# Two engines without work wait for the last load instead of ending at once, in a ReLU-and-row-sum kernel

## The chip, the cores and the metric

The kernel runs on one core of a Trainium2 chip. The metric is the device time of one execution in microseconds; lower is better. Every execution also has a span: the time from the first to the last instruction of the kernel in its profile. The device time was 1.3 to 1.7 us longer than the span in the kernels that nothing held up at their end, and this case is about what lies in that difference. All executions quoted here were at a granted clock of 1.0.

## The reference

```python
def setup_inputs():
    batch, seq, dim = 32, 512, 1024
    return {"x": np.random.randn(batch, seq, dim).astype(np.float32)}

def reference(x):
    relu_x = np.maximum(x, 0)
    return np.sum(relu_x, axis=-1).astype(np.float32)
```

The input is 32 x 512 x 1024 x 4 bytes = 67.1 MB, the output 64 KB. Every input byte is read once.

## The kernel before

SyncE issues all loads and stores. ScalarE and VectorE do the arithmetic. TensorE and GpSimd get no work, apart from four small constant fills on GpSimd and the barrier at the start, both of which the framework adds. Seven loads of 8.39 MB go through three buffers; the rest is loaded in shrinking pieces, so that little is left to compute when the last piece lands.

```python
    n_in = NBIG + len(TAIL) + 2
    s_in = [nc.alloc_semaphore(f"s_in{i}") for i in range(n_in)]   # one for each load
    # ... the other semaphores ...
    for c in range(NBIG + 1):
        if c >= NB:
            sp.wait_ge(s_dve, 3 * (c - NB + 1))        # buffer free again
        if c < NBIG:
            g, j = CHUNKS[c]
            sp.dma_start(out=buf[:, c % NB, :, :], in_=xv[g][:, j : j + BIG, :]).then_inc(
                s_in[c], 16
            )
    # ... the shrinking loads; the last one: ...
    sp.dma_start(out=last[:, 0 : LAST[1]], in_=xv[-1][:, BIG - 1, LAST[0] : D]).then_inc(
        s_in[-1], 16
    )
    # ... wait for two flags, then the first store (112 of 128 columns) ...

    # ... ScalarE: relu, VectorE: sum, for six big loads; after that rows are shared out ...
    act.wait_ge(s_in[-2], 16)
    on_act(buf[:, tb, BIG - 1, 0 : LAST[0]], last[:, LAST[1] : LAST[1] + 1]).then_inc(s_tact, 1)
    dve.wait_ge(s_tact, 1)
    dve.wait_ge(s_in[-1], 16)
    on_dve(last[:, :], res[:, J - 1 : J]).then_inc(s_tdve, 1)

    sp.wait_ge(s_tdve, 1)
    sp.dma_start(out=ov[-1][:, :], in_=res[:, start[-1] : J]).then_inc(s_out, 16)
    sp.wait_ge(s_store, 16 * (len(REGIONS) - 1))
    sp.wait_ge(s_out, 16)
```

Of the kernel before, what the change touches and what calls it, by code (L numbers as in the profile page):

```python
# [2 lines left out]

P = 128
D = 1024
BIG = 16
NTWO = 6
NB = 3
REGIONS = [112, 16]
CHUNKS = [(0, 0), (0, 16), (0, 32), (0, 48), (0, 64), (0, 80), (0, 96)]  # L10
STEPS = [4, 5, 7]
MIXED = [3, 4, 5]
TAIL = [8, 4, 2, 1]
LAST = [512, 512]


def bass_relu_sum_kernel(
    nc: bass.Bass,
    x: bass.AP,
    out: bass.AP,  # L20
):







    fp32 = mybir.dt.float32
    ALU = mybir.AluOpType  # L30
    AF = mybir.ActivationFunctionType
    X = mybir.AxisListType.X

    B, S, _ = x.shape
    J = B * S // P
    NBIG = len(CHUNKS)
    assert BIG * NBIG + sum(TAIL) + 1 == J == sum(REGIONS) and sum(LAST) == D

    xr = x.rearrange("b s d -> (b s) d")
    of = out.rearrange("b s -> (b s)")  # L40
    start = [sum(REGIONS[:i]) for i in range(len(REGIONS))]
    xv = [
        xr[P * s : P * (s + n), :].rearrange("(p j) d -> p j d", p=P)
        for s, n in zip(start, REGIONS)
    ]
    ov = [of[P * s : P * (s + n)].rearrange("(p j) -> p j", p=P) for s, n in zip(start, REGIONS)]

    buf = nc.alloc_sbuf_tensor("buf", [P, NB, BIG, D], fp32)
    last = nc.alloc_sbuf_tensor("last", [P, LAST[1] + 1], fp32)
    res = nc.alloc_sbuf_tensor("res", [P, J], fp32)  # L50

    n_in = NBIG + len(TAIL) + 2
    s_in = [nc.alloc_semaphore(f"s_in{i}") for i in range(n_in)]
    s_act = nc.alloc_semaphore("s_act")
    s_dve = nc.alloc_semaphore("s_dve")
    s_fact = nc.alloc_semaphore("s_fact")
    s_fdve = nc.alloc_semaphore("s_fdve")
    s_tact = nc.alloc_semaphore("s_tact")
    s_tdve = nc.alloc_semaphore("s_tdve")
    s_store = nc.alloc_semaphore("s_store")  # L60
    s_out = nc.alloc_semaphore("s_out")

    sp, act, dve = nc.sync, nc.scalar, nc.vector


    tb = NBIG % NB
    for c in range(NBIG + 1):
        if c >= NB:
            sp.wait_ge(s_dve, 3 * (c - NB + 1))
# [5 lines that stand above are left out]
    r = 0  # L75
    tail = []
    for i, n in enumerate(TAIL):
        sp.dma_start(out=buf[:, tb, r : r + n, :], in_=xv[-1][:, r : r + n, :]).then_inc(  # L78
            s_in[NBIG + i], 16
        )  # L80
        tail.append((r, n, s_in[NBIG + i]))
        r += n
    sp.dma_start(out=buf[:, tb, r, 0 : LAST[0]], in_=xv[-1][:, BIG - 1, 0 : LAST[0]]).then_inc(
        s_in[-2], 16
    )
    sp.dma_start(out=last[:, 0 : LAST[1]], in_=xv[-1][:, BIG - 1, LAST[0] : D]).then_inc(
        s_in[-1], 16
    )
    sp.wait_ge(s_fact, 1)
    sp.wait_ge(s_fdve, 1)  # L90
    for g in range(len(REGIONS) - 1):
        sp.dma_start(
            out=ov[g][:, :], in_=res[:, start[g] : start[g] + REGIONS[g]]
        ).then_inc(s_store, 16)


    def on_act(t, acc):
        return act.activation(t, t, AF.Relu, accum_out=acc)  # L98

    def on_dve(t, acc):  # L100
        return dve.tensor_scalar(  # L101
            out=t, in0=t, scalar1=0.0, scalar2=None, op0=ALU.max, op1=ALU.add, accum_out=acc
        )

    def row(c, i):
        return buf[:, c % NB, i, :], res[:, c * BIG + i : c * BIG + i + 1]

    for c in range(NTWO):
        b, steps = c % NB, STEPS if c < NTWO - 1 else MIXED
        act.wait_ge(s_in[c], 16)  # L110
        if steps is MIXED:
            dve.wait_ge(s_in[c], 16)
            for i in (BIG - 4, BIG - 3):
                on_dve(*row(c, i))
        r = 0
        for i, n in enumerate(steps):
            t = buf[:, b, r : r + n, :]
            act.activation(t, t, AF.Relu).then_inc(s_act, 1)  # L118
            dve.wait_ge(s_act, 3 * c + i + 1)
            dve.tensor_reduce(  # L120
                out=res[:, c * BIG + r : c * BIG + r + n], in_=t, axis=X, op=ALU.add
            ).then_inc(s_dve, 1)
            r += n
        if steps is MIXED:
            for i in (BIG - 2, BIG - 1):
                on_act(*row(c, i))


    j0 = NBIG * BIG
    for c in range(NTWO, NBIG):  # L130
        act.wait_ge(s_in[c], 16)
        dve.wait_ge(s_in[c], 16)
        for i in range(BIG):
            ins = (on_act if i % 2 else on_dve)(*row(c, i))
            if i >= BIG - 2:
                ins.then_inc(s_fact if i % 2 else s_fdve, 1)
    for r, n, s in tail:
        if n > 1:
            act.wait_ge(s, 16)
        dve.wait_ge(s, 16)  # L140
        for i in range(r, r + n):
            f = on_act if (i - r) % 2 else on_dve
            f(buf[:, tb, i, :], res[:, j0 + i : j0 + i + 1])
# [14 lines that stand above are left out]
# [1 line left out]
_INS = ['x']  # L159
_OUTS = [((32, 512), 'float32')]  # L160


# [21 lines left out]
```

## Time and profile before

| | before |
|---|---|
| device time, median of 3 | 162.47 us (162.46 to 162.5) |
| span of the profiled execution | 160.7 us |
| device time of the same execution | 162.37 us |
| DMA queue, share of 16 engines' span | 97.4% |
| VectorE, ScalarE busy | 76%, 63% |

The page of the profile, lines of its parts 1 and 3 (busy time and share of the span; packets, MB, share of the engines):

```profile
span 160.7 us, 145 instructions
...
DVE 122.0 (76%) x56; ACT 101.0 (63%) x55; POOL 0.2 (0%) x4
...
q1 hardware_dynamic: 2160, 67.18, 97.4%
HBM read 67.11 MB, written 0.07 MB: 418 GB/s over the span
```

The queue has work nearly all the time. TensorE does not appear, and GpSimd (POOL) has 0.2 us of work at the start. So the loads bound the kernel. The chain of work that ended last is made of loads for the most part. Some 27% of it is ScalarE and VectorE, since SyncE issues a load only when VectorE has freed its buffer; the loads issued before it keep the queue at work meanwhile. The columns are start, length and what it was:

```profile
by line: DMA buf<-in_x_dram 69.2%; ACT buf L118 17.5%; DVE res L120 9.5%; SPq L78 1.0%; ACT buf L98 0.5%; DVE last L101 0.4%; issue 0.3%; SPq L72 0.2%
...
1.17 40.75 DMA buf<-in_x_dram
...
41.94 14.05 ACT buf L118 x3
...
56.01 7.63 DVE res L120
...
63.66 36.31 DMA buf<-in_x_dram
...
123.55 34.19 DMA buf<-in_x_dram
157.74 0.02 issue
157.76 0.73 ACT buf L98 x2
158.49 0.03 issue
158.53 0.69 DVE last L101 x2
```

The timeline of the last two microseconds (start, length, engine, line, operation) and SyncE's longest wait there:

```profile
157.76 0.63 ACT L98 ACTIVATE buf<-buf 128x512 f32<-128x512 f32 x1 [0.83 <-DMA buf<-in_x_dram]
...
158.53 0.69 DVE L101 TENSOR_SCALAR_CACHE_REDUCE last<-last 128x513 f32<-128x513 f32 x1 [0.21 <-ACT buf L98]
159.14 0.08 DVE L101 DVE_READ_ACCUMULATOR last<-last 128x1 f32 x1
159.25 0.34 SPq L153 DMA_DIRECT2D out_dram<-res  x1
```
```profile
SPq L155 <- DMA out_dram<-res: 1.1, 1, 1.1
```

After the last load there is one short reduction and the last store; SyncE then waits 1.1 us for the store, and the span ends at 160.71.

The profile's views stop there, but the trace's semaphore records go on. A semaphore is a counter that engines and transfers count up and that engines wait on; the records show when each one was counted up or cleared. Semaphore 2 belongs to the system's barrier. These are its counts in the trace of before, after the kernel's start, in us:

```
first barrier, way in:   0.943  158.593  158.631  159.367  160.829
first barrier, way back: 160.873  160.911  160.945  160.994
all semaphores from 7 to 255 cleared, in five groups: 160.954 to 161.720
second barrier:          161.810  161.844  161.883  161.927  161.950  162.049  162.087  162.121  162.168
```

The Trainium skill, page "Runtime: NRT & Kernel Launch", section "The ~15µs preamble/postamble breakdown", describes the barrier ahead of a kernel as a chain through the five engines with about 44 ns for each of 8 hops (a hop is the step from one count to the next), and lists for the end of a kernel a barrier, a reset of the semaphores and another barrier. The trace agrees in form: there are nine counts, which is one for each engine on the way in and one for each of the first four on the way back, and the hops of the way back are 34 to 49 ns. An engine counts only when the engine before it in the chain has counted. ScalarE's last instruction ended at 158.485, VectorE's at 159.222 and SyncE's at 160.712; the counts at 158.593, 159.367 and 160.829 follow these by 0.11 to 0.15 us. The counts at 0.943 and 158.631 are then those of the two engines without work.

### The profile page before, as it was taken

How to read it: one execution, taken by the hardware profiler on the slowest of the kernel's cores; microseconds unless marked ns; L12 is line 12 of the kernel's file. 1: busy time of each engine (PE TensorE's matmuls, PEld its weight loads, DVE VectorE, ACT ScalarE, POOL GpSimd, SP SyncE). 2: the span in 40 equal slices, each digit the busy share in tenths (PEclk: the TensorE clock that was granted, in tenths of full speed). 3: DMA queues.
4: the chain of work that ended last, by engine and by line, in shares of the span. 5: the costliest groups of instructions: out<-in, count | busy, mean ns of one | idle time of the engine just before them, and what ended most of it. 6: DMA issues, size and time to landing. Idle time of an engine off the chain costs nothing.

```text
span 160.7 us, 145 instructions
## 1 busy us (share of the span) xinstructions
DVE 122.0 (76%) x56; ACT 101.0 (63%) x55; POOL 0.2 (0%) x4
## 2 busy tenths in 40 slices
DVE  0000004998969898898969989699899999598995
ACT  3000039991599907997099951999329980496972
POOL 0000000000000000000000000000000000000000
DMA  8969969969969969969969969969969969899993
GB/s 261 522 261 522 522 261 522 522 261 522 522 261 522 522 261 522 522 261 522 522 261 522 522 261 522 522 261 522 522 261 522 506 277 522 367 416 391 418 399 113
DMA packets 2160, 67.18 MB, mean 418 GB/s; under 512 B 496, under 2 KB 496, under 8 KB 880
## 3 DMA queue, kind: packets, MB, share of 16 engines
q1 hardware_dynamic: 2160, 67.18, 97.4%
HBM read 67.11 MB, written 0.07 MB: 418 GB/s over the span
## 4 chain that ended last, share of the span: by engine, by line
DMA 69%; ACT 18%; DVE 10%; SPq 1%; issue 0%
DMA buf<-in_x_dram 69%; ACT buf L118 17%; DVE res L120 9%; SPq L78 1%; ACT buf L98 0%; DVE last L101 0%; SPq L72 0%
## 5 line engine op out<-in xcount | busy, mean ns | idle before, releaser
L120 DVE TENSOR_REDUCE res<-buf 128x4 f32<-128x4096 f32 (+3 forms) x18 | 100.4, 5604 | 34.3 <-ACT buf L118 34.3
L118 ACT ACTIVATE buf<-buf 128x4096 f32<-128x4096 f32 (+3 forms) x18 | 80.8, 4553 | 47.1 <-DMA buf<-in_x_dram 47.1
L98 ACT ACTIVATE buf<-buf 128x1024 f32<-128x1024 f32 (+1 forms) x18 | 18.4, 1021 | 9.7 <-DMA buf<-in_x_dram 9.7
L101 DVE TENSOR_SCALAR_CACHE_REDUCE buf<-buf 128x1024 f32<-128x1024 f32 x18 | 21.0, 1215 | 2.7 <-DMA buf<-in_x_dram 2.5
L98 ACT ACTIVATION_READ_ACCUMULATOR buf<-buf 128x1 f32 x18 | 3.4, 186 | 0.0
L118 ACT ACT_TABLE_LOAD x1 | 1.3, 1283 | 0.7 <-PEq L169 0.7
L101 DVE DVE_READ_ACCUMULATOR buf<-buf 128x1 f32 x18 | 1.5, 83 | 0.0
L101 DVE TENSOR_SCALAR_CACHE_REDUCE last<-last 128x513 f32<-128x513 f32 x1 | 0.7, 690 | 0.2 <-ACT buf L98 0.2
L169 POOL MEMSET const-bfloat16-1.0<- 128x1 bf16 x1 | 0.1, 102 | 0.0
L169 POOL MEMSET const-uint8-127<- 128x1 uint8 x1 | 0.1, 102 | 0.0
L169 POOL MEMSET const-float32-0.0<- 128x1 f32 x1 | 0.1, 99 | 0.2 <-issue 0.2
L169 POOL MEMSET const-float32-1.0<- 128x1 f32 x1 | 0.1, 99 | 0.0
L101 DVE DVE_READ_ACCUMULATOR last<-last 128x1 f32 x1 | 0.1, 83 | 0.0
## 6 DMA issues: line engine op xcount, KB each, us to landing
buf<-in_x_dram SPq DMA_DIRECT2D x1, 4096.0 KB, 26.7
buf<-in_x_dram SPq DMA_DIRECT2D x1, 2048.0 KB, 31.2
buf<-in_x_dram SPq DMA_DIRECT2D x1, 1024.0 KB, 33.2
buf<-in_x_dram SPq DMA_DIRECT2D x1, 512.0 KB, 34.0
buf<-in_x_dram SPq DMA_DIRECT2D x1, 256.0 KB, 34.2
last<-in_x_dram SPq DMA_DIRECT2D x1, 256.0 KB, 34.3
buf<-in_x_dram SPq DMA_DIRECT2D x7, 36.3
out_dram<-res SPq DMA_DIRECT2D x1, 56.0 KB, 10.6
```

Of the source, the lines that this page charges most:

```text
L78: sp.dma_start(out=buf[:, tb, r : r + n, :], in_=xv[-1][:, r : r + n, :]).then_inc(s_in[NBIG + i], 16)
L98: return act.activation(t, t, AF.Relu, accum_out=acc)
L101: return dve.tensor_scalar(out=t, in0=t, scalar1=0.0, scalar2=None, op0=ALU.max, op1=ALU.add, accum_out=acc)
L118: act.activation(t, t, AF.Relu).then_inc(s_act, 1)
L120: dve.tensor_reduce(out=res[:, c * BIG + r : c * BIG + r + n], in_=t, axis=X, op=ALU.add).then_inc(s_dve, 1)
L169: nc = _bacc.Bacc("TRN2", target_bir_lowering=False, num_devices=1)
```

## The change

Its intent: TensorE and GpSimd, which have nothing to do, should not run on to the end of their streams while the loads are on, but wait inside the kernel until the last load has landed.

```diff
@@ after the first store is issued
             out=ov[g][:, :], in_=res[:, start[g] : start[g] + REGIONS[g]]
         ).then_inc(s_store, 16)
 
+    for idle in (nc.tensor, nc.gpsimd):
+        idle.wait_ge(s_in[-1], 16)
```

Nothing else changes. The order of instructions on every engine is the same, and the program has one more instruction on each of the two engines. Line numbers of the changed kernel are shifted by 1 to 4.

## The prediction

> What bounds the kernel. Loads do. The page of the profile gives the one DMA queue 97.4% of the 160.7 us span and 418 GB/s; VectorE is busy 76%, ScalarE 63%. In the trace's semaphore records the 8.39 MB chunks complete 19.35 us apart (22.1, 41.45, 60.8, ... us), which is 433.6 GB/s. The Trainium skill ("DMA: Bandwidth & Descriptors", section "Where 436 GB/s comes from") names 435.2 GB/s as the ceiling of the ports into on-chip memory; the trace agrees. After the last load only a short tail remains (timeline): the last load is complete at 158.41, VectorE's last work runs 158.53 to 159.22, the store is issued at 159.25, complete at 160.67, and SyncE's final wait ends the span at 160.71. The reported time of the profiled run is 162.37 us.
>
> What the change does. It removes nothing and adds one semaphore wait to TensorE and one to GpSimd. The instruction order on VectorE, ScalarE and SyncE and all loads stay as they were. The two engines write no buffer, so no buffer comes free at another time and no transfer moves. A released wait of this kind takes 17 to 51 ns in the trace (start barrier).
>
> What it can touch: only the closing sequence that the system runs after the kernel. The Trainium skill ("Runtime: NRT & Kernel Launch", section "The ~15us preamble/postamble breakdown") lists a barrier over the five engines that passes from engine to engine at about 44 ns a hop, a reset of the semaphores, and another barrier. The trace shows it. The barrier's semaphore is counted up at 0.94 us (one engine that had nothing to do), 158.593 (108 ns after ScalarE's last instruction), 158.631 (the other idle engine, 38 ns later), 159.367 (145 ns after VectorE's last), 160.829 (117 ns after SyncE's last), then back in hops of 34 to 49 ns until 160.994; semaphores are cleared from 160.95 to 161.72, and the second barrier runs from 161.81 to 162.17.
>
> On the critical path? With the change the two idle engines are released at 158.41, when the last load's semaphore reaches 16, plus about 30 ns (VectorE's own wait on that semaphore ended at 158.435), and reach the barrier some 0.15 us later, an estimate from the 108 to 145 ns seen above: about 158.55 to 158.60. ScalarE gets there at 158.593, so the first three steps move by 0 to 0.1 us. VectorE arrives only at 159.367 and SyncE at 160.829, so there are about 0.7 and 2.2 us of slack. Nothing of it reaches the end. Waiting at one semaphore instead of at the barrier's frees no resource that the kernel uses.
>
> Predicted time: 162.45 us, range 162.15 to 162.8; the rest is scatter between runs (before: 0.04 us) and chips, and possibly a tenth of a microsecond if the closing sequence starts differently. Faster by over 2%: 1%; within 2%: 98%; slower by over 2%: 1%.
>
> What would show it right or wrong. Span 160.6 to 160.8 us, chunk spacing 19.35 us, the tail's 158.41 to 160.71 unchanged within 0.1 us, two new waits ending near 158.45 on TensorE and GpSimd; the barrier's first count moves from 0.94 to about 158.6, its fifth stays about 0.12 us after SyncE's last wait, and reported time less span stays about 1.7 us.
>
> What would make it wrong: [...] the engine that clears its semaphores last (161.43 to 161.72) starts sooner or later because it waited elsewhere; or engines that end at once disturb the loads in a way that this trace doesn't show, which the chunk spacing near the ceiling speaks against.

## The result, and the profile after

| | before | after |
|---|---|---|
| device time, median of 6 | 162.47 us (162.19 to 162.53) | 162.21 us (161.94 to 162.4) |
| ratio of the fast runs | | 0.9988, 95% interval 0.9975 to 1.0001 |
| span of the profiled execution | 160.7 us | 160.6 us |
| first load complete | 22.584 us | 22.436 us |
| last load complete | 158.407 us | 158.260 us |
| last store complete | 160.668 us | 160.516 us |
| first barrier's fifth count, after the store | 0.161 us | 0.161 us |
| second barrier's last count, after the store | 1.500 us | 1.503 us |

A ratio here compares the mean times of the fast runs, so it is not quite the ratio of the medians. The last five rows are from the semaphore records. The six executions of before hold the three of the table further up (162.46 to 162.5 us); the other three took 162.53, 162.19 and 162.26 us, a median of 162.26.

The interval just holds 1. The page of after:

```profile
span 160.6 us, 147 instructions
...
DVE 122.0 (76%) x56; ACT 100.9 (63%) x55; POOL 0.2 (0%) x4
...
q1 hardware_dynamic: 2160, 67.18, 97.4%
HBM read 67.11 MB, written 0.07 MB: 418 GB/s over the span
```

The chain that ended last, after:

```profile
by line: DMA buf<-in_x_dram 69.2%; ACT buf L122 17.5%; DVE res L124 9.5%; SPq L79 1.1%; ACT buf L102 0.5%; DVE last L105 0.4%; issue 0.3%; SPq L73 0.2%
...
1.16 40.61 DMA buf<-in_x_dram
...
41.80 14.05 ACT buf L122 x3
...
55.87 7.63 DVE res L124
...
63.52 36.30 DMA buf<-in_x_dram
...
123.43 34.16 DMA buf<-in_x_dram
157.60 0.02 issue
157.62 0.73 ACT buf L102 x2
158.35 0.03 issue
158.38 0.69 DVE last L105 x2
```

The timeline of its end and SyncE's wait:

```profile
157.62 0.63 ACT L102 ACTIVATE buf<-buf 128x512 f32<-128x512 f32 x1 [0.81 <-DMA buf<-in_x_dram]
...
158.38 0.69 DVE L105 TENSOR_SCALAR_CACHE_REDUCE last<-last 128x513 f32<-128x513 f32 x1 [0.21 <-ACT buf L102]
158.99 0.08 DVE L105 DVE_READ_ACCUMULATOR last<-last 128x1 f32 x1
159.10 0.34 SPq L157 DMA_DIRECT2D out_dram<-res  x1
```
```profile
SPq L159 <- DMA out_dram<-res: 1.1, 1, 1.1
```

The two extra instructions are the two waits (147 instead of 145). Every line of the tail is 0.14 to 0.15 us earlier, with the same lengths. The shift was already there in the first piece of the chain: the first load completed 0.148 us earlier (22.436 against 22.584), and the spacing of the loads after that is the same (19.34 to 19.37 us after, 19.33 to 19.36 before). So the difference between these two spans (0.15 us) arose in the first 22 us, where the waits had not ended yet, and not at the end, where they do end. The device times of the two executions differ by 0.24 us (162.37 and 162.13); the other 0.09 us lies outside the span, and the records do not show where.

The barrier's counts after the change:

```
first barrier, way in:   158.531  158.565  158.839  159.219  160.677
first barrier, way back: 160.720  160.759  160.793  160.840
second barrier:          161.662  161.696  161.735  161.778  161.801  161.900  161.938  161.972  162.019
```

The count at 0.943 has gone to 158.531 as it should. The third count now comes 0.274 us after the second, where before it followed by 0.038 us: GpSimd arrives late. Its wait ended at 158.302 and it counted 0.537 us later; TensorE's ended at 158.341 and it counted 0.190 us later. But VectorE counted at 159.219 and SyncE at 160.677, so this lateness was absorbed. From the store's completion to the end of the second barrier, the two traces agree within 3 ns. Why GpSimd needs longer than TensorE, no run here shows.

Two questions are open at this point. Is the 0.26 us between the medians a gain or scatter? And is the change free because of the slack at the barrier, or because waiting costs nothing anywhere?

### The profile page after: what moved, and what is told of

It is laid out like the page before. It is cut to its first block, busy times and chain, and to the rows that moved or that the text cites. A ratio compares the mean times of both kernels' runs of the same rounds, so it can differ in the third digit from the quotient of the medians.

```text
span 160.6 us, 147 instructions
## 1 busy us (share of the span) xinstructions
DVE 122.0 (76%) x56; ACT 100.9 (63%) x55; POOL 0.2 (0%) x4
## 3 DMA queue, kind: packets, MB, share of 16 engines
q1 hardware_dynamic: 2160, 67.18, 97.4%
## 4 chain that ended last, share of the span: by engine, by line
DMA 69%; ACT 18%; DVE 10%; SPq 1%; issue 0%
DMA buf<-in_x_dram 69%; ACT buf L122 18%; DVE res L124 10%; SPq L79 1%; ACT buf L102 0%; DVE last L105 0%; SPq L73 0%
```

## The experiments

All kernels gave the correct result. All were run in five rounds, in three sets, each set on one chip with nine executions of the kernel before: the a runs, the b and d runs (both on chip 1), and the c runs (chip 13). The theory: the change is hidden behind VectorE's and SyncE's later arrival at the barrier, and the 0.26 us is scatter of the first load. The rivals: a small real gain in the first load; or waiting is free wherever it ends.

### Nothing added (a1_nothing)

```diff
-    for idle in (nc.tensor, nc.gpsimd):
-        idle.wait_ge(s_in[-1], 16)
+    # no wait on the idle engines
```

> The two waits are left out again, so the program is that of before with its lines shifted: the noise floor of this comparison. Both theories: ratio to before within 0.998 to 1.002, difference of medians under 0.2 us. Theory (the 0.26 us by which the changed kernel was measured faster is scatter): the first load's completion may lie anywhere from 22.4 to 22.7 us. Rival (idle engines that end at once disturb the first load): it completes at 22.55 us or later, as in before (22.584), not at 22.44 as in the changed kernel.

Measured: median 162.38 us (162.13 to 162.45), before 162.24 us (162.06 to 162.45), ratio 1.0006, interval 0.9992 to 1.002. First load complete at 22.603 us. The same program thus differs from itself by 0.14 us in the medians. Also, before had 162.47 us as its median in the first comparison and 162.24 us here. A difference of 0.26 us is therefore not far from the scatter, but one trace with the first load at 22.603 did not yet reject the rival.

### The change again (a2_again)

```diff
     for idle in (nc.tensor, nc.gpsimd):
         idle.wait_ge(s_in[-1], 16)
```

> The change as it was, repeated. Theory (scatter, nothing on the critical path): median within 0.15 us of the run with nothing added, span 160.6 to 160.8 us, interval holds 1. Rival (the wait really saves some 0.15 to 0.26 us): median 0.15 us or more below it, interval wholly under 1, first load complete at 22.44 again.

Measured: median 162.23 us (161.95 to 162.31), ratio 0.9996, interval 0.9983 to 1.0008. The median lies 0.15 us below that of the run with nothing added, which is the boundary of what was expected of the rival, and the first load was complete at 22.475 us. Against before's own nine runs (162.24 us) there is no difference. Inconclusive at a tenth of a microsecond; it was followed up below.

### Waiting for the first load only (a4_first_load)

```diff
-        idle.wait_ge(s_in[-1], 16)
+        idle.wait_ge(s_in[0], 16)
```

> The idle engines wait for the first load alone (about 22 us) and then end. Theory: as before, difference under 0.15 us; barrier counts at about 22.7 us for TensorE, then 158.6 for ScalarE. Rival a (engines that end at once disturb the first load): faster by 0.15 us, as much as the change, first load complete at 22.44. Rival b (engines that stand at the closing barrier disturb the later loads): load spacing as in before and no gain, while the change gains.

Measured: median 162.14 us (162.04 to 162.46), ratio 0.9997, interval 0.9985 to 1.001; first load complete at 22.549 us, barrier counts 22.820 and 158.549. The time is that of before. The first load's completion lies between the two values that the theories were to be told apart by, so this run does not settle the first load. It shows no harm to the later loads from engines that stand at the barrier: the spacing stays 19.32 to 19.36 us.

### Waiting for the final store (a3_all_done)

```diff
-        idle.wait_ge(s_in[-1], 16)
+        idle.wait_ge(s_out, 16)
```

> The idle engines wait for the final store's semaphore instead, so they come to the closing barrier at the very end, with no slack. In the changed kernel GpSimd needed 0.58 us from the semaphore to its count at the barrier (158.26 to 158.84) and TensorE 0.27. Theory (the change is free because it is hidden behind VectorE's and SyncE's arrival): the last count of the barrier's way out comes about 0.6 us after the store's completion instead of 0.16, so the time grows by 0.4 to 0.6 us (ratio 1.0025 to 1.004), with the span as it was or up to 0.1 us longer. Rival (waiting costs nothing wherever it ends): no growth, under 0.15 us.

Measured: median 162.87 us (162.56 to 163.04), ratio 1.0035, interval 1.0023 to 1.0048. By means that is 162.826 - 162.256 = 0.57 us more, within the 0.4 to 0.6 us expected. The timeline to the store is as it was, only with a slower first load (22.717 us) ahead of it:

```profile
span 160.9 us, 147 instructions
```
```profile
158.66 0.69 DVE L105 TENSOR_SCALAR_CACHE_REDUCE last<-last 128x513 f32<-128x513 f32 x1 [0.20 <-ACT buf L102]
159.28 0.08 DVE L105 DVE_READ_ACCUMULATOR last<-last 128x1 f32 x1
159.39 0.34 SPq L157 DMA_DIRECT2D out_dram<-res  x1
```
```profile
SPq L159 <- DMA out_dram<-res: 1.1, 1, 1.1
```

Of the cost, 0.54 us is behind the store's completion; the rest, 0.03 us, is less than the scatter of the spans. The store was complete at 160.801, and the barrier's counts were:

```
first barrier:  161.072  161.106  161.380  161.424  161.447  161.545  161.583  161.617  161.664
second barrier: ... 162.844
```

TensorE counts 0.271 us after the store, GpSimd 0.579 us after it, and VectorE and SyncE, whose own work is done, only follow. The end comes 2.043 us after the store instead of 1.500. Waiting is not free where there is no slack, so the second rival falls, and the change's own cost is absorbed only because it ends early enough.

### Which engine makes the end late (d1_pe_all_done, d2_pool_all_done)

```diff
-    for idle in (nc.tensor, nc.gpsimd):
-        idle.wait_ge(s_in[-1], 16)
+    for idle in (nc.tensor,):            # d1; d2: (nc.gpsimd,)
+        idle.wait_ge(s_out, 16)
```

> TensorE alone waits for the final store. Theory (the late engine's own way from semaphore to barrier, then the hops behind it): TensorE counts 0.27 us after the store's completion, the others follow in hops of 34, 38, 44 and 23 ns, SyncE at 0.41 us, turn of 0.10 us; the last count of the second barrier comes 1.80 us after the store instead of 1.50, time longer by 0.3 us. Rival (the cost is that of the late GpSimd alone): no growth.

Measured: median 162.59 us (162.51 to 162.81), ratio 1.0022, interval 1.001 to 1.0035; by means 162.650 - 162.281 = 0.37 us more. The end of the second barrier comes 1.806 us after the store, so 0.31 us of it are the barrier, as expected. The other 0.06 us are within the scatter: the nine executions of before alone cover 0.35 us. Of the longer mean span (160.80 against 160.71) 0.035 us is TensorE's own wait, which now ends after SyncE's.

> GpSimd alone waits for the final store. Theory: GpSimd counts 0.58 us after the store's completion, last count of the second barrier 2.04 us after it as with both engines, time longer by 0.54 us. Rival (the costs of both engines add up): 0.27 us or less for GpSimd alone.

Measured: median 162.83 us (162.65 to 163.04), ratio 1.0036, interval 1.0024 to 1.0049; by means 162.874 - 162.281 = 0.59 us more; the end 2.037 us after the store. GpSimd alone costs as much as both engines together (0.57 us). The costs do not add: the later of the two hides the other. The counts also settle who is who. With GpSimd alone late the first count stays at 0.942 and the third moves; with TensorE alone late the first moves. So TensorE counts first and GpSimd third.

### Waiting for VectorE's result (b3_result_ready)

```diff
-        idle.wait_ge(s_in[-1], 16)
+        idle.wait_ge(s_tdve, 1)
```

> The idle engines wait for VectorE's last result (complete 1.4 us before the final store's semaphore). Theory (hidden as long as the latest idle engine, GpSimd at 0.58 us after its semaphore, counts before SyncE): GpSimd counts at about 159.8 us, VectorE's count moves from 159.4 to about 159.85, SyncE's stays 0.16 us after the store's completion; last count of the second barrier stays 1.50 us after the store; time within 0.15 us of before. Rival (any later arrival is added to the time): 0.3 us or more longer.

Measured: median 162.38 us (162.32 to 162.43), ratio 1.0006, interval 0.9993 to 1.0018. By means that is 0.10 us above before, as much as the run with nothing added was above it (162.354 against 162.256), so it is within the noise. GpSimd counted at 159.831 and VectorE right behind it at 159.874, half a microsecond later than in before; SyncE at 160.844, still 0.160 us after the store. The end comes 1.505 us after the store. Here VectorE was held up by GpSimd, and the time still did not change beyond the noise, because SyncE comes last. That is the slack seen directly: the cost starts only when the chain of the idle engines reaches SyncE after its own arrival.

### The change a third time, and in turn with nothing (b4_third, c1, c2)

These are the same two programs as above. The edits are none and that of the first experiment.

> The change as it was, a third time, because its span read about 0.1 us under that of before in both sets of runs so far. Theory (how long the first load takes differs from execution to execution and is not tied to the change): span 160.65 to 160.85, mean within 0.1 us of before, interval holds 1. Rival (a real gain of about 0.1 us in the first load): mean span 160.65 or less against 160.75 of before, mean time 0.1 us or more below, the third time in a row.

Measured: median 162.3 us (162.07 to 162.36), ratio 0.9998, interval 0.9985 to 1.0012. Mean time 162.266 us against 162.281 of before. Mean span 160.66 against 160.71. This meets what the theory expected, but the span only just (160.65 was the rival's limit), so it was put to a last test.

> Change and no change in turn on one chip, two sets of five each, to settle a residue of 0.1 us: so far 16 executions with the change have mean spans of 160.63 to 160.68 us, those without 160.71 to 160.76. Theory (scatter of the first load): the two sets with the change and the two without overlap, and the difference of the means of ten is under 0.08 us. Rival (a small real gain): both sets with the change lie 0.08 us or more below both without, in the time and in the span.

> No wait on the idle engines, first set. Theory: mean time within 0.08 us of the sets with the change. Rival: 0.08 us or more above both.

> The change, second set. Theory and rival as for the first set.

> No wait on the idle engines, second set. Theory and rival as for the first set; the difference from the first set of the same program is the scatter between two loads of one program.

| five runs each | median us | ratio to before | mean us | mean span us | first load, profiled run |
|---|---|---|---|---|---|
| c1_change | 162.3 | 0.9999 (0.9986 to 1.0011) | 162.280 | 160.68 | 22.597 |
| c1_nothing | 162.18 | 0.9998 (0.9984 to 1.0011) | 162.242 | 160.70 | 22.594 |
| c2_change | 162.34 | 1.0001 (0.9988 to 1.0013) | 162.314 | 160.74 | 22.359 |
| c2_nothing | 162.31 | 0.9997 (0.9984 to 1.001) | 162.250 | 160.66 | 22.495 |
| before, nine runs | 162.29 | | 162.299 | 160.76 | |

The two sets with the change lie 0.03 to 0.07 us above those without. The residue has changed its sign, and the rival of a gain of 0.08 us or more fails its own test. Taken together, the four repeats of the change (20 executions) have a mean of 162.261 us, and the six sets without it in the same three comparisons (42 executions) 162.280 us. That is a difference of 0.02 us, a hundredth of one per cent, with a standard error of 0.035 us from the scatter of these executions. A gain of a few hundredths of a microsecond is thus not excluded.

The semaphore records of all 14 traces, in us:

| kernel | idle engines wait for | store complete | fifth count after it | end of the second barrier after it |
|---|---|---|---|---|
| before | nothing | 160.668 | 0.161 | 1.500 |
| after | last load | 160.516 | 0.161 | 1.503 |
| a1_nothing | nothing | 160.726 | 0.160 | 1.502 |
| a2_again | last load | 160.556 | 0.161 | 1.504 |
| b4_third | last load | 160.591 | 0.161 | 1.503 |
| a4_first_load | first load | 160.612 | 0.161 | 1.500 |
| b3_result_ready | VectorE's result | 160.684 | 0.160 | 1.505 |
| c1_change | last load | 160.684 | 0.160 | 1.503 |
| c1_nothing | nothing | 160.651 | 0.161 | 1.499 |
| c2_change | last load | 160.436 | 0.161 | 1.504 |
| c2_nothing | nothing | 160.572 | 0.161 | 1.504 |
| d1_pe_all_done | store, TensorE alone | 160.836 | 0.410 | 1.806 |
| d2_pool_all_done | store, GpSimd alone | 160.826 | 0.645 | 2.037 |
| a3_all_done | store, both | 160.801 | 0.646 | 2.043 |

Read the last two columns: they are constant to 6 ns as long as SyncE arrives last, and only the last three kernels differ. The third column scatters by 0.4 us, and follows the first load. The device time has a scatter besides: in the eleven profiled executions with the constant end it was 1.34 to 1.70 us longer than the span. These 0.36 us are neither in the span nor between the store and the end of the second barrier, and the traces do not show where they are. So the first load is only a part of the scatter of the device time.

## Why the prediction was right

- **The loads bound the kernel, and the change does not touch them.** Right. The queue's share is 97.4% in both, and the spacing of the big loads is the same within 0.02 us, 19.35 us on average. The Trainium skill, page "DMA: Bandwidth & Descriptors", section "Where 436 GB/s comes from", gives 435.2 GB/s for the ports into on-chip memory; 8.39 MB in 19.35 us is 433.4 to 433.7 GB/s, here and in all runs (from each trace's own mean spacing), so the trace agrees with the figure. That it is the ports that hold the loads to it, no run here shows.
- **Only the closing barrier can notice.** Right, and shown by three kernels that do make it notice: they add 0.37 to 0.59 us, all but some hundredths of it in the barrier.
- **There is slack.** Right. The prediction gave 0.7 us to VectorE and 2.2 us to SyncE. In the changed kernel GpSimd's count came 0.38 us before VectorE's (158.839 and 159.219), and waiting for VectorE's result used up VectorE's slack without any change of the time.
- **The engines need about 0.15 us from the wait to the barrier.** Wrong in size. From the semaphore to the count it was 0.27 us for TensorE and 0.58 us for GpSimd. The prediction took ScalarE's, VectorE's and SyncE's 0.11 to 0.15 us, with 0.03 us for the wait's release, for all engines. "The first three steps move by 0 to 0.1 us" failed in the third: GpSimd's count comes 0.58 us after the last load, where in before the third count came 0.22 us after it. The second just failed too: 0.31 us instead of 0.19. Since the slack was larger, nothing followed for the time. Where the engines wait for the store and there is no slack, this term alone would have made GpSimd's count about 0.4 us too early (an estimate: 0.58 us measured less the 0.18 us assumed).
- **What would show it right or wrong.** Two of these marks were missed. The tail was to stay unchanged within 0.1 us and came 0.15 us earlier, with the first load. Device time less span was to stay about 1.7 us and was 1.57 us (162.13 less 160.56). Neither comes from the barrier, whose fifth count came 0.12 us after SyncE's wait, as predicted.
- **The predicted 162.45 us** is 0.24 us above the first median (162.21) and 0.11 to 0.22 us above the four repeats (162.23 to 162.34), all inside the stated range. The part that was off is the starting value: before itself, 162.46 to 162.5 us in the first three executions, had medians of 162.24 to 162.29 us in the later sets.

What stays open is why the first load completes anywhere from 22.36 to 22.77 us. It is not tied to the change, since kernels with it show 22.36 to 22.60 and those without 22.50 to 22.60, and it makes up nearly all of the scatter of the profiled spans: span less first load is 138.10 to 138.17 us in all 14. Whether the three slowest (22.72 to 22.77), all in kernels with a late barrier, are chance was not tested. The spans of all 15 executions of these three kernels average 160.79 us, against 160.71 us for the other 43 executions of the a, b and d runs on the same chip. In two of the three, 0.035 us of this is only TensorE's wait, which ends last. The rest, about 0.05 us, is less than twice its standard error of 0.03 us and settles nothing.

## What to carry to other kernels

In this kernel, an engine that has nothing to do cost nothing measurable by ending early and gained nothing by waiting; what counts at the end is which engine comes last to the closing barrier. If an idle engine must wait, let it be for something that is over about 0.6 us before the last engine is done, above all on GpSimd. The 0.6 us are an estimate from GpSimd's 0.58 us; the runs tried 1.4 us, which was free, and none, which cost 0.57 us, and nothing between. For a difference of a tenth of a per cent, run the unchanged program as an experiment too, and look in the trace for where the difference begins: here the part that the trace shows began in the first load, while the two engines stood waiting in both kernels.

## What the Trainium skill lacked or had wrong

- "Runtime: NRT & Kernel Launch", the preamble/postamble breakdown: it gives a hop of the barrier, but not how long an engine takes from the end of its last wait to its count. The runs show 0.12 us for SyncE, 0.19 us for TensorE and 0.54 us for GpSimd (from the semaphore itself: 0.27 us for TensorE and 0.58 us for GpSimd, the same within 1 ns in every trace where it was read).
- The same page: about 44 ns a hop over 8 hops. As a mean this agrees: the second barrier's eight hops in the trace of before take 0.358 us, 45 ns each. Single hops differ, which the page doesn't say: 34 to 49 ns for most, but 23 to 24 ns from VectorE to SyncE and 97 to 99 ns for SyncE's turn when it was ready early.
- The same page gives about 1.5 us for the closing reset of the semaphores and 2 us for the barrier and the rearming of the DMA after it. In the trace of before the clearing took 0.77 us (160.954 to 161.720), about half of the page's figure. The second barrier's counts ended 0.45 us after that, but the records don't show the rearming, so the 2 us are not tested here.
- No page has the spread of a first load: 22.36 to 22.77 us to its completion over 14 traces, while the big loads behind it came 19.31 to 19.37 us apart.
